# Adding gathered rows four gathers later, with seven row buffers, in the last stage of a transformer block

## The chip, the cores and the metric

One core of a Trainium2 chip runs the whole program. The metric is the device time of one execution in microseconds (us), the median of several runs. The core has five engines with a queue of instructions each: TensorE (PE, with PEld for its weight loads), VectorE (DVE), ScalarE (ACT), GpSimd (POOL) and SyncE (SP, which only issues DMAs here). Each engine takes its instructions in their order, and waits at one whose inputs or buffers are not ready.

## The reference

The program is one layer of a streaming encoder over 256 tokens of width 2048: two mixers, an output projection, and then a layer of very many small experts (PEER), and a final normalisation. The last stage computes the output half of the experts:

```
eidx, gate = top 16 of 128 x 128 experts, for each of 8 heads     # 128 experts for each token
a  = einsum('td,thkd->thk', x, emb_u[eidx])
w  = gelu(a) * gate
y  = einsum('thk,thkd->td', w, emb_v[eidx])                       # the last stage
x  = x + ga2 * y
out = rmsnorm(x, norm_f_g)
```

`emb_v` has 16384 rows of 2048 float32 numbers, 134 MB.

## The kernel before, in words

Tokens lie on partitions in two groups of 128 (`tt` is 0 or 1). The stages up to the experts' weights are not touched by the change. What is left is y, and the columns of y are computed in two ways side by side.

Columns 576 to 2047 (`GV` = 1472 of them) are a dense product. An earlier step scattered the weights w into a table `W` (the same memory as `A`), 128 blocks of 128 experts by 256 tokens, zero where a token did not choose an expert. For each of the 128 blocks (`NK`) `v_load` brings 128 rows of the table `v_cols` by an SP DMA into a buffer `vb` (three of them, 736 KB each) and splits them into a high and a low part: ACT casts `vb` to `vh` (L1079), DVE subtracts to get `vl` (L1081). The weights of the block are split the same way (`wh` L1075, `wl` L1077). `vh` and `vl` have two buffers each. The PE then does 18 matmuls a block, in three runs of six, `wh` x `vh`, `wl` x `vh` and `wh` x `vl` (`product`, L1131): they add into six banks `yp` over all 128 blocks. A `vb` buffer is free for the next load once its `vl` is written.

Columns 0 to 575 (`GW` = 576) are gathered: for each of the 256 pairs of a token group and one of its 128 chosen experts, an indirect DMA issued from POOL (`gather`, L755) fetches a row for each of the 128 tokens into a buffer `gat`, and DVE multiplies it with the weight and adds it to `yg` (L1064, L1062 for the first of a group). In `weigh`, before, both are one step: the gather is recorded and then its addition. There are five `gat` buffers, and a new gather waits for the addition that read its buffer.

The main loop runs over blocks i. It records the load and split of block i + 1, then the products of block i, then two gathers with their additions (256 gathers over 124 blocks are 2.06 a block). Each gather is held back until the last product of block i (`after=mm`). The order in which each engine meets the work is set by the program's scheduler, which keeps the dependencies and otherwise goes by a priority that follows the recorded order.

At the end (`residual` and `finish`) DVE multiplies `yg` and `yp` with `ga2`, adds x, and after a normalisation SP stores the result.

Of the kernel before, what the change touches and what calls it, by code (L numbers as in the profile page):

```python
# [10 lines left out]
F32 = mybir.dt.float32  # L11
F32R = mybir.dt.float32r
# [3 lines left out]
AF = mybir.ActivationFunctionType  # L16
ALU = mybir.AluOpType
PACE = mybir.DependencyInfo(mybir.DependencyClass.Sync, mybir.DependencyReason.DATA)
AX = mybir.AxisListType
PSUM = bass.MemoryType.PSUM  # L20

P = 128
T = 256
# [37 lines left out]
GW = 576  # L61
ON_POOL = ((0, 3), (1, 3))
BACK, ENDS = NK - 5, 4
COLS = 2 * NK - 50
GV = D - GW

# [48 lines left out]
def block_kernel(ctx, tc, a, out):  # L115
    nc = tc.nc
    def pool(name, side, bufs=1, space=None):
        stack = ExitStack()
        kw = {} if space == bass.MemoryType.DRAM else {"reuse_waits": "tile"}
        if space is not None:  # L120
            kw["space"] = space
        return stack.enter_context(tc.tile_pool(name=name, bufs=bufs, side=side, **kw)), stack

    keep, keep_s = pool("keep", "left")
# [3 lines left out]
    late = {}  # L128
# [26 lines left out]
    first = sb.tile([P, 4 * D], F32, tag="oT", name="first")  # L155
# [11 lines left out]
    def rsqrt(dst, src, scale):  # L167
        nc.vector.tensor_scalar(dst, src, scale, EPS, op0=ALU.mult, op1=ALU.add)
        nc.vector.reciprocal(dst, dst)
        nc.scalar.activation(dst, dst, AF.Sqrt)  # L170
# [121 lines left out]
    def first_products(j, w, parts, last=False, after=None):  # L292
        for part in parts:
            for c in range(3):
                for tt in range(TT):
                    acc, ww, cs = (qacc[c * TT + tt], w[0], c * WIDE) if c < 2 else (kacc[tt], w[1], 0)
                    for k in range(2):
# [3 lines left out]
                        if after is not None:  # L301
                            tc.add_manual_dep(mm.ins, after.ins.name, PACE, reason="the modulation first")

# [392 lines left out]
    u_rows, u_cols, v_rows, v_cols = a["peer_u_rows"], a["peer_u_cols"], a["peer_v_rows"], a["peer_v_cols"]  # L696
# [16 lines left out]
    def norm2():  # L713
        drain()
        nc.sync.dma_start(ga2d, adaR[96:97])
        ssum = late["ssum"] = keep.tile([P, TT], F32, name="ssum")
        nc.vector.tensor_reduce(ssum, late["ss"], axis=AX.X, op=ALU.add)
        rsqrt(ssum, ssum, 1.0 / D)
# [29 lines left out]
    def rows_of(name):  # L748
        return pe[name].rearrange("p t h k -> p t (h k)")
# [3 lines left out]
    def gather(pool_, tag, table, width, bufs, tt, n, after=None, room=None):  # L753
        g = pool_.tile([P, room or width], F32, tag=tag, bufs=bufs, name="gat")[:, :width]
        d = nc.gpsimd.indirect_dma_start(out=g, out_offset=None, in_=table,  # L755
                                         in_offset=bass.IndirectOffsetOnAxis(ap=rows_of("idx")[:, tt, n:n + 1], axis=0))
        if after is not None:
            tc.add_manual_dep(d.ins, after.ins.name, PACE, reason="gathers spread over the products")
        return g
# [12 lines left out]
    todo = [(tt, n) for hs in range(0, HEADS, 2) for tt in range(TT) for n in range(hs * TOPK, (hs + 2) * TOPK)]  # L772
# [8 lines left out]
    def route_post(h):  # L781
        def post(ps):
# [61 lines left out]
            nc.gpsimd.tensor_tensor(oh, oh, idf.rearrange("p t q k -> p (t q) k")[:, :, None, :].to_broadcast(every), op=ALU.mult)  # L844
            nc.vector.tensor_reduce(got, oh.rearrange("p (t q) k a -> p t q k a", q=2), axis=AX.X, op=ALU.add)
            nc.vector.scalar_tensor_tensor(pe["idx"][:, :, h], got[:, :, 0], float(NK), got[:, :, 1], op0=ALU.mult, op1=ALU.add)
# [11 lines left out]
    drain()  # L858
    i12 = pe["i12"].rearrange("p t q h k -> p q t (h k)")
    idx, gate = rows_of("idx"), rows_of("gate")  # L860
    colT = keep.tile([P, 4, T], F32, name="colT")
    i1T, i2T, wT, gT = (colT[:, i] for i in range(4))
    wrow = pe["wrow"]
    neg = keep.tile([P, T], F32, name="neg")
    idr = keep.tile([P, P], F32R, name="idr")

    def softmax():
        ex = pe["gate"]
# [3 lines left out]
        nc.scalar.activation(ex, ex, AF.Exp)  # L872
        nc.vector.tensor_reduce(sm, ex, axis=AX.X, op=ALU.add)
        nc.vector.reciprocal(sm, sm)
        nc.vector.tensor_tensor(ex, ex, sm[:, :, :, None].to_broadcast([P, TT, HEADS, TOPK]), op=ALU.mult)

    def columns():
        softmax()
        nc.scalar.copy(idr, ident)
        for dst, src in ((i1T, i12[:, 0]), (i2T, i12[:, 1]), (gT, gate)):  # L880
            pt = bank("pt")
            for tt in range(TT):
                nc.tensor.transpose(pt[:, tt * P:(tt + 1) * P], src[:, tt], ident)
            nc.scalar.copy(dst, pt[:, :T])
            if dst is i2T:
                nc.scalar.mul(neg, pt[:, :T], -1.0)
# [23 lines left out]
    for n in range(DIRECT):  # L910
        mm = u_products(n)
    late["pg_s"].close()
    st_s.close()
    big, big_s = pool("big", "left")
    A = big.tile([P, NK, T], F32, tag="big", name="A")

    rate = (len(todo) - LEFT) / (2 * NK - PRE)
    done = 0
    for n in range(2 * NK):
        if n >= DIRECT:  # L920
            mm = u_products(n)
        if n % 4 == 3:
            nc.scalar.copy(A[:, n // 2 - 1:n // 2 + 1], sums.pop(n // 4))
        if n == COLS:
            columns()
# [49 lines left out]
    def pick(u):  # L975
        for h in range(2):
# [3 lines left out]
            for t in range(4):  # L980
                mm = nc.tensor.matmul(pkv[:, t], oh[:, t], A[:, :, t0 + t], start=True, stop=True)
                tc.declare_no_dep(mm.ins, group="scattered", reason="other tokens' columns")
# [11 lines left out]
    def scatter(u):  # L994
# [3 lines left out]
        for h in range(0, SET, 4):  # L998
            pw, pwv = psum("pw", 3)
            for t in range(4):  # L1000
                nc.tensor.matmul(pwv[:, t], o2[:, h + t].bitcast(F32), o1[:, h + t], start=True, stop=True)  # L1001
            put = nc.scalar.copy(A[:, :, t0 + h:t0 + h + 4].rearrange("p n t -> p t n"), pwv)  # L1002
            tc.add_to_no_dep_group("scattered", put.ins)
# [20 lines left out]
    for u in range(-LEAD, units + LAG):  # L1024
        if 0 <= u < units and u % half == 0:
            tt = u // half
# [18 lines left out]
        if 0 <= u < units and u % half == half - 1:  # L1045
            pt, _ = psum("pk", 3)
            nc.tensor.transpose(pt[:, :P], wT[:, tt * P:(tt + 1) * P], ident)
            nc.vector.tensor_copy(wrow[:, tt], pt[:, :P])
    W = A

    p2_s.close()
    pq_s.close()
    py, py_s = pool("py", "left", bufs=1, space=PSUM)
    psc, psc_s = pool("psc", "left", bufs=2, space=PSUM)
    p3, p3_s = pool("p3", "right")

    yg = p3.tile([P, TT, GW], F32, name="yg")
    def weigh(tt, n, after=None):
        g = gather(p3, "gat", v_rows, GW, 5, tt, n, after)
        w = wrow[:, tt, n:n + 1]  # L1060
        if n == 0:
            nc.vector.tensor_scalar(yg[:, tt], g, w, None, op0=ALU.mult)  # L1062
        else:
            nc.vector.scalar_tensor_tensor(yg[:, tt], g, w, yg[:, tt], op0=ALU.mult, op1=ALU.add)  # L1064

    todo = list(pairs)
    chunks = [(c, min(512, GV - c)) for c in range(0, GV, 512)]
# [2 lines left out]
    def v_load(i):  # L1070
        room, bufs = (p3, 1) if i % 3 == 2 else (pv, 2)
        vb = room.tile([P, GV], F32, tag="vb", bufs=bufs, name="vb")
        nc.sync.dma_start(vb, v_cols[i * P:(i + 1) * P])
        wh = p3.tile([P, T], F32R, tag="wh", bufs=3, name="wh")
        nc.scalar.copy(wh, W[:, i])  # L1075
        wl = p3.tile([P, T], F32R, tag="wl", bufs=3, name="wl")
        nc.vector.tensor_tensor(wl, W[:, i], wh.bitcast(F32), op=ALU.subtract)  # L1077
        vh = p3.tile([P, GV], F32R, tag="vh", bufs=2, name="vh")
        nc.scalar.copy(vh, vb)  # L1079
        vl = p3.tile([P, GV], F32R, tag="vl", bufs=2, name="vl")  # L1080
        late["split"] = nc.vector.tensor_tensor(vl, vb, vh.bitcast(F32), op=ALU.subtract)  # L1081
        return vh, vl, wh, wl

    spent = A.rearrange("p n t -> p (n t)")
    x1 = spent[:, :TT * D].rearrange("p (t d) -> p t d", t=TT)
# [7 lines left out]
    def restore(after):  # L1093
# [6 lines left out]
        for d in loads:  # L1100
            tc.add_manual_dep(d.ins, after.ins.name, PACE, reason="behind the last of the table")

    def residual(tt, m):
        c, w, n = parts[m]
        xs = xo[:, tt, c:c + w]
        mul = nc.vector.tensor_tensor(xs, yg[:, tt] if n is None else yp[tt][n][:, :w], ga2[:, c:c + w], op=ALU.mult)  # L1106
        tc.add_manual_dep(mul.ins, late["split"].ins.name, PACE, reason="the last operands first")
        (nc.gpsimd if (tt, m) in ON_POOL else nc.vector).tensor_tensor(xs, xs, x1[:, tt, c:c + w], op=ALU.add)  # L1108
        nc.scalar.activation(sq[:, :w], xs, AF.Square, accum_out=ss3[:, tt, m:m + 1])
        if n is None:  # L1110
            nc.gpsimd.tensor_tensor(xs, xs, gf[:, c:c + w], op=ALU.mult)

    def finish(tt):
        for m in range(len(chunks)):
            residual(tt, m)
        r = rf[:, tt:tt + 1]
        nc.vector.tensor_reduce(r, ss3[:, tt], axis=AX.X, op=ALU.add)
        rsqrt(r, r, 1.0 / D)
# [18 lines left out]
    for i in range(NK - 2):  # L1137
        ops = nxt
        nxt = v_load(i + 1)
        for j in range(3):  # L1140
            for tt in range(TT):
                for n in range(len(chunks)):
                    mm = product(i, ops, j, tt, n)
        while todo and done < rate * (i + 1):
            weigh(*todo.pop(0), after=mm)
            done += 1
        if i == BACK:
            restore(mm)
    ends = [nxt, v_load(NK - 1)]
    for tt in range(TT):  # L1150
        residual(tt, len(parts) - 1)
    for tt in range(TT):
# [61 lines left out]
```

## Time and profile before

| | us |
|---|---|
| three runs | 2393.7, 2394.3, 2401.22 |
| median | 2394.3 |
| span of the profiled execution | 2393.9 |
| last stage, from the first `vh` cast (1803.31) to the end | 590.6 |

The page gives no other time for the profiled execution than its span. In the page's first part an engine's busy time and its share of the span stand side by side: PE 2208.9 us (92%), DVE 1785.1 us (75%), ACT 1031.0 us (43%), POOL 874.9 us (37%). These are means over stages with different limits. In a row of a group of instructions the numbers after the bar are the time in which at least one of them ran, the mean duration of one in ns, and the idle time of that engine just before them with what ended it. In a timeline a row is a start, a duration, an engine, a line and an operation, and in brackets the time its engine stood idle before it and what ended that.

### The profile page before, as it was taken

To read this page: it belongs to the slowest core of one execution; us is meant where nothing else is said; L and a number is where in the kernel's file an instruction comes from. 1 tells how busy PE (TensorE), PEld (TensorE's weight loads), DVE (VectorE), ACT (ScalarE), POOL (GpSimd) and SP (SyncE) were. 2 spreads that over 40 slices of the span, in tenths; PEclk is the share of its full clock that TensorE was granted. 3 is DMA by queue.
4 is the path that set the end of the run, shared out by engine and by line. 5 is a ranking of instruction groups with operands and counts; after the bars stand their busy time and mean duration, and the time that the engine had idled before them with its cause. 6 is when DMAs were issued, how large, how long until landed. Compare 5 with 4: busy or idle time off the path is not lost. (4 is left out here: it accounts for less than half of the span.)

```text
span 2393.9 us, 37307 instructions
## 1 busy us (share of the span) xinstructions
PE 2208.9 (92%) x13988; PEld 1949.2 (81%) x13988; DVE 1785.1 (75%) x3416; ACT 1031.0 (43%) x1440; POOL 874.9 (37%) x750
## 2 busy tenths in 40 slices
PE   6999999999999998893999999989998998998996
PEld 3577779999999888783889999989997777777775
DVE  3478878888788755787767777777766877877777
ACT  3245556643344444101444444457774333333333
POOL 0000000000000002766444444467775665666664
PEclk9999999999999999996999999999999999999998
DMA  9977778777777765767999999971107888888987
GB/s 353 380 296 265 273 267 297 276 286 283 285 295 282 264 213 180 257 224 221 302 302 313 318 316 313 305 248 54 33 1 253 310 301 297 304 306 299 313 310 269
DMA packets 144312, 638.26 MB, mean 267 GB/s; under 512 B 20721, under 2 KB 26625, under 8 KB 112001
## 3 DMA queue, kind: packets, MB, share of 16 engines
q1 hardware_dynamic: 102146, 459.65, 53.7%
q0 software_dynamic: 41984, 176.23, 21.8%
q8 instruction: 109, 1.79, 0.3%
q14 instruction: 73, 0.60, 0.1%
HBM read 631.59 MB, written 4.20 MB: 266 GB/s over the span
## 5 line engine op out<-in xcount | busy, mean ns | idle before, releaser
L755 POOL DMA_INDIRECT gat<-in_peer_v_rows,eidx x256 | 351.4, 1373 | 211.3 <-PE yp L1131 138.7
L755 POOL DMA_INDIRECT gat<-in_peer_u_rows,eidx x256 | 315.0, 1230 | 301.8 <-DVE ulo L710 146.2
L211 ACT CAST whi<-wt 128x2048 fp32r<-128x2048 f32 x130 | 248.0, 1908 | 292.4 <-PE mm L412 224.4
L906 PE MATMUL mmu<-h2T,uhi 128*128 128x256 f32 x2360 | 323.9, 284 | 33.6 <-ACT uhi L709 33.6
L762 DVE SCALAR_TENSOR_TENSOR gat<-gat,h2b 128x768 f32<-128x768 f32 x256 | 245.1, 959 | 142.9 <-DMA gat<-in_peer_u_rows,eidx 141.6
L213 DVE TENSOR_TENSOR wlo<-wt,whi 128x2048 fp32r<-128x2048 f32 (+1 forms) x130 | 292.3, 2249 | 55.5 <-ACT whi L211 51.6
L906 PEld LDWEIGHTS mmu<-h2T,uhi 128*128 128x128 f32 x2360 | 301.8, 193 | 34.4 <-ACT uhi L709 34.4
L1079 ACT CAST vh<-vb 128x1472 fp32r<-128x1472 f32 x128 | 182.9, 1429 | 340.6 <-DMA vb<-in_peer_v_cols 289.4
L356 POOL DMA_DIRECT2D br<-in_b_ada x32 | 15.8, 493 | 773.2 <-DVE ada_acc L357 726.8
L1064 DVE SCALAR_TENSOR_TENSOR yg<-gat,wrow,yg 128x576 f32<-128x576 f32 x254 | 207.5, 817 | 113.0 <-DMA gat<-in_peer_v_rows,eidx 110.8
L709 ACT CAST uhi<-ub 128x640 fp32r<-128x640 f32 x236 | 171.5, 728 | 268.3 <-DMA ub<-in_peer_u_cols 220.8
L1131 PE MATMUL yp<-vl,wh 128*128 128x512 f32 (+1 forms) x768 | 201.3, 396 | 45.9 <-DVE vl L1081 45.0
L353 DVE SCALAR_TENSOR_TENSOR ada_acc<-wa,sc_col,ada_acc 128x256 f32<-128x256 f32 x480 | 231.7, 483 | 11.4
L1081 DVE TENSOR_TENSOR vl<-vb,vh 128x1472 fp32r<-128x1472 f32 x128 | 215.6, 1684 | 6.6 <-ACT vh L1079 6.6
L906 PE MATMUL mmu<-h2T,ulo 128*128 128x256 f32 x1180 | 188.1, 290 | 32.1 <-DVE ulo L710 30.7
L1131 PEld LDWEIGHTS yp<-vl,wh 128*128 128x128 f32 x768 | 139.1, 189 | 96.0 <-DVE vl L1081 72.8
L906 PEld LDWEIGHTS mmu<-h2T,ulo 128*128 128x128 f32 x1180 | 158.2, 192 | 45.8 <-DVE ulo L710 44.7
L1131 PE MATMUL yp<-vh,wh 128*128 128x512 f32 (+1 forms) x768 | 192.2, 384 | 2.6 <-ACT wh L1075 2.6
L710 DVE TENSOR_TENSOR ulo<-ub,uhi 128x640 fp32r<-128x640 f32 x236 | 188.8, 820 | 6.2 <-ACT uhi L709 5.8
L1131 PE MATMUL yp<-vh,wl 128*128 128x512 f32 (+1 forms) x768 | 191.4, 383 | 0.1
L412 PE MATMUL mm<-whi,hT 128*128 128x512 f32 (+1 forms) x832 | 181.7, 362 | 0.0
L1131 PEld LDWEIGHTS yp<-vh,wh 128*128 128x128 f32 x768 | 145.0, 189 | 28.4 <-ACT wh L1075 2.8
(275 smaller groups left out, 3696.2 us busy)
## 6 DMA issues: line engine op xcount, KB each, us to landing
wa<-in_w_ada SPq DMA_DIRECT2D x96, 1024.0 KB
vb<-in_peer_v_cols SPq DMA_DIRECT2D x128, 736.0 KB
ub<-in_peer_u_cols SPq DMA_DIRECT2D x256, 320.0 KB
wt<-in_w_vg SPq DMA_DIRECT2D x32, 1024.0 KB
wt<-in_w_branch_gate SPq DMA_DIRECT2D x32, 1024.0 KB
wt<-in_w_u SPq DMA_DIRECT2D x16, 1024.0 KB
wt<-in_w_b_out SPq DMA_DIRECT2D x16, 1024.0 KB
wt<-in_w_o SPq DMA_DIRECT2D x16, 1024.0 KB
```

The costliest lines, as they stand in the source:

```text
L211: nc.scalar.copy(hi, wt)
L213: nc.vector.tensor_tensor(lo[:, :cut], wt[:, :cut], hi[:, :cut].bitcast(F32), op=ALU.subtract)
L353: nc.vector.scalar_tensor_tensor(acc, wt[:, k], s, acc, op0=ALU.mult, op1=ALU.add)
L412: nc.tensor.matmul(job.ps[b], l, r, start=(first and k == 0 and i == 0 and not lo_part), stop=(last and k == job.rows - 1 and lo_part == 1))
L710: (nc.gpsimd if n < POOL else nc.vector).tensor_tensor(lo[:, :w], ub[:, :w], hi[:, :w].bitcast(F32), op=ALU.subtract)
L755: d = nc.gpsimd.indirect_dma_start(out=g, out_offset=None, in_=table, in_offset=bass.IndirectOffsetOnAxis(ap=rows_of("idx")[:, tt, n:n + 1 ...
L762: nc.vector.scalar_tensor_tensor(g, g, 1.0, h2b[:, tt, :UG], op0=ALU.mult, op1=ALU.mult, accum_out=pe["wrow"][:, tt, n:n + 1])
L906: mm = nc.tensor.matmul(acc, w[:, k - k0], x, start=(first and k == 0 and i == 0), stop=(last and k == FK - 1 and i == len(steps) - 1))
L1064: nc.vector.scalar_tensor_tensor(yg[:, tt], g, w, yg[:, tt], op0=ALU.mult, op1=ALU.add)
L1079: nc.scalar.copy(vh, vb)
L1081: late["split"] = nc.vector.tensor_tensor(vl, vb, vh.bitcast(F32), op=ALU.subtract)
L1131: return nc.tensor.matmul(yp[tt][n][:, :w], l[:, tt * P:(tt + 1) * P], r[:, c:c + w], start=(i == 0 and j == 0), stop=(i == NK - 1 and j = ...
```

## The change

A gather and its addition are parted. `fly` issues the gather and puts it on a list; `weigh` takes the oldest of the list and adds it, and is called while more than `BEHIND` = 4 gathers are on the list. So in block i the additions are those of the gathers that were issued two blocks before. An ordering edge without a semaphore (`QUEUED`) puts each addition behind `late["split"]`, the `vl` of block i + 1. The buffers `gat` are seven in place of five (2304 bytes a partition each). Their room comes from three tables of the stage before (`colT`, `neg`, `idr`, 4096 + 1024 + 512 bytes a partition), which now lie in a pool of their own that is closed before the last stage. What is still on the list after the loop is added behind the load of the last block.

```diff
+VG, BEHIND = 7, 4
...
-    colT = keep.tile([P, 4, T], F32, name="colT")
-    i1T, i2T, wT, gT = (colT[:, i] for i in range(4))
-    neg = keep.tile([P, T], F32, name="neg")
-    idr = keep.tile([P, P], F32R, name="idr")
...
+    pick_room, pick_room_s = pool("pickroom", "left")
+    colT = pick_room.tile([P, 4, T], F32, name="colT")
+    i1T, i2T, wT, gT = (colT[:, i] for i in range(4))
+    neg = pick_room.tile([P, T], F32, name="neg")
+    idr = pick_room.tile([P, P], F32R, name="idr")
...
+    pick_room_s.close()
...
-    def weigh(tt, n, after=None):
-        g = gather(p3, "gat", v_rows, GW, 5, tt, n, after)
+    flying = []
+
+    def fly(tt, n, after):
+        flying.append((gather(p3, "gat", v_rows, GW, VG, tt, n, after), tt, n))
+
+    def weigh():
+        g, tt, n = flying.pop(0)
         w = wrow[:, tt, n:n + 1]
         if n == 0:
-            nc.vector.tensor_scalar(yg[:, tt], g, w, None, op0=ALU.mult)
+            d = nc.vector.tensor_scalar(yg[:, tt], g, w, None, op0=ALU.mult)
         else:
-            nc.vector.scalar_tensor_tensor(yg[:, tt], g, w, yg[:, tt], op0=ALU.mult, op1=ALU.add)
+            d = nc.vector.scalar_tensor_tensor(yg[:, tt], g, w, yg[:, tt], op0=ALU.mult, op1=ALU.add)
+        tc.add_manual_dep(d.ins, late["split"].ins.name, QUEUED, reason="the split of the next block first")
...
         while todo and done < rate * (i + 1):
-            weigh(*todo.pop(0), after=mm)
+            fly(*todo.pop(0), after=mm)
             done += 1
+        while len(flying) > BEHIND:
+            weigh()
         if i == BACK:
             restore(mm)
     ends = [nxt, v_load(NK - 1)]
+    while flying:
+        weigh()
```

DVE's queue before, in the middle of the stage. `vl_19133` and `vl_19167` belong to blocks 40 and 41; `gat_19085` and `gat_19088` are the two gathers held back until the last product of block 37, `gat_19119` and `gat_19122` those of block 38, `gat_19153` the first of block 39.

```order
L1064 SCALAR_TENSOR_TENSOR yg_17770<-gat_19085,wrow_8619,yg_17770 128x576
L1064 SCALAR_TENSOR_TENSOR yg_17770<-gat_19088,wrow_8619,yg_17770 128x576
L1081 TENSOR_TENSOR vl_19133<-vb_19125,vh_19131 128x1472
L1077 TENSOR_TENSOR wl_19163<-A_9902,wh_19161 128x256
L1064 SCALAR_TENSOR_TENSOR yg_17770<-gat_19119,wrow_8619,yg_17770 128x576
L1064 SCALAR_TENSOR_TENSOR yg_17770<-gat_19122,wrow_8619,yg_17770 128x576
L1081 TENSOR_TENSOR vl_19167<-vb_19159,vh_19165 128x1472
L1077 TENSOR_TENSOR wl_19197<-A_9902,wh_19195 128x256
L1064 SCALAR_TENSOR_TENSOR yg_17770<-gat_19153,wrow_8619,yg_17770 128x576
```

The same place of DVE's queue now. The `vl` of a block has the same number; the gathers of block 37 are `gat_19085` and `gat_19087`, those of block 38 `gat_19119` and `gat_19121`, and `vl_19201` belongs to block 42.

```order
L1091 TENSOR_TENSOR vl_19133<-vb_19125,vh_19131 128x1472
L1073 SCALAR_TENSOR_TENSOR yg_17774<-gat_19085,wrow_8619,yg_17774 128x576
L1087 TENSOR_TENSOR wl_19163<-A_9899,wh_19161 128x256
L1073 SCALAR_TENSOR_TENSOR yg_17774<-gat_19087,wrow_8619,yg_17774 128x576
L1091 TENSOR_TENSOR vl_19167<-vb_19159,vh_19165 128x1472
L1073 SCALAR_TENSOR_TENSOR yg_17774<-gat_19119,wrow_8619,yg_17774 128x576
L1087 TENSOR_TENSOR wl_19197<-A_9899,wh_19195 128x256
L1073 SCALAR_TENSOR_TENSOR yg_17774<-gat_19121,wrow_8619,yg_17774 128x576
L1091 TENSOR_TENSOR vl_19201<-vb_19193,vh_19199 128x1472
```

The gathers of block 37 stood ahead of the `vl` of block 40 and now stand behind it; those of block 38 stood ahead of the `vl` of block 41 and now stand ahead of that of block 42. Each `vl` waits for gathers that were issued one block earlier than before, and an addition now stands on each side of the `wl`.

The end of DVE's queue before: the last two additions and the last two `vl`, then the first step of the residual.

```order
L1064 SCALAR_TENSOR_TENSOR yg_17770<-gat_22024,wrow_8619,yg_17770 128x576
L1064 SCALAR_TENSOR_TENSOR yg_17770<-gat_22027,wrow_8619,yg_17770 128x576
L1081 TENSOR_TENSOR vl_22070<-vb_22062,vh_22068 128x1472
L1077 TENSOR_TENSOR wl_22094<-A_9902,wh_22092 128x256
L1081 TENSOR_TENSOR vl_22098<-vb_22090,vh_22096 128x1472
L1106 TENSOR_TENSOR A_9902<-yg_17770,A_9902 128x576 x2
```

And now (`vl_22098` is the `vl` of the last block, `gat_21990` and `gat_21992` the first two of the last four gathers):

```order
L1091 TENSOR_TENSOR vl_22070<-vb_22062,vh_22068 128x1472
L1087 TENSOR_TENSOR wl_22094<-A_9899,wh_22092 128x256
L1091 TENSOR_TENSOR vl_22098<-vb_22090,vh_22096 128x1472
L1073 SCALAR_TENSOR_TENSOR yg_17774<-gat_21990,wrow_8619,yg_17774 128x576
L1116 TENSOR_TENSOR A_9899<-yg_17774,A_9899 128x576
L1073 SCALAR_TENSOR_TENSOR yg_17774<-gat_21992,wrow_8619,yg_17774 128x576
```

The last four additions moved behind the last `vl`, in among the steps of the residual. On POOL, SP and PE the order in the stage is as it was (the stores of the result come in another order). On ACT the cast that fills `idr` moved from the start of the program, with a table load of its own, to the stage that needs it.

## Rows read from the trace of the kernel before

**Rows 1.** Page: the chain that ended last, by line, shares of the span.

```profile
DMA gat<-in_peer_v_rows,eidx 12%; POOL gat L755 3%; DVE yg L1064 2%; DVE vl L1081 1%; PE yp L1131 1%; DMA vb<-in_peer_v_cols 1%; DVE wl L1077 0%; DVE A L1108 0%; ACT vh L1079 0%; DVE A L1106 0%; DVE A L1124 0%; POOLq L755 0%; PE pw L1001 0%; ACT A L1002 0%; DVEq L1064 0%
```

**Rows 2.** Windows: busy time of each engine from 1850 to 2250 us.

```profile
core 0: us, PE busy (x) PEld busy (x) DVE busy (x) ACT busy (x) POOL busy (x), PEclk, DMA share, GB/s
1850.00:2250.00 400.00, 367.48 (x1605) 297.66 (x1604) 316.27 (x363) 153.15 (x177) 253.86 (x186) 1.00 0.88 304
```

**Rows 3.** Groups by line, 1850 to 2340 us: busy, mean ns, idle before.

```profile
L755 POOL DMA_INDIRECT gat<-in_peer_v_rows,eidx x226 | 312.9, 1384 | 180.4 <-PE yp L1131 124.8 <-issue 25.0 <-DVE yg L1064 20.8
L1081 DVE TENSOR_TENSOR vl<-vb,vh 128x1472 fp32r<-128x1472 f32 x110 | 185.2, 1684 | 0.0
L1064 DVE SCALAR_TENSOR_TENSOR yg<-gat,wrow,yg 128x576 f32<-128x576 f32 x224 | 183.0, 817 | 101.2 <-DMA gat<-in_peer_v_rows,eidx 99.3
L1131 PE MATMUL yp<-vl,wh 128*128 128x512 f32 (+1 forms) x654 | 170.6, 396 | 39.6 <-DVE vl L1081 38.8 <-issue 0.2
...
L1079 ACT CAST vh<-vb 128x1472 fp32r<-128x1472 f32 x109 | 155.7, 1429 | 298.2 <-DMA vb<-in_peer_v_cols 258.9 <-PE yp L1131 23.4 <-DVE yg L1064 6.9
```

**Rows 4.** Timeline: the `vl` of block 5 and that of block 125.

```profile
1827.47 1.74 DVE L1081 TENSOR_TENSOR vl<-vb,vh 128x1472 fp32r<-128x1472 f32 x1
...
2364.03 1.69 DVE L1081 TENSOR_TENSOR vl<-vb,vh 128x1472 fp32r<-128x1472 f32 x1
```

**Rows 5.** Timeline, 1977 to 1997 us: a gather that keeps PE waiting.

```profile
1978.48 1.48 PE L1131 MATMUL yp<-vh,wh 128*128 128x512 f32 x6
1978.84 1.68 DVE L1081 TENSOR_TENSOR vl<-vb,vh 128x1472 fp32r<-128x1472 f32 x1
...
1978.92 2.43 POOL L755 DMA_INDIRECT gat<-in_peer_v_rows,eidx  x1 [2.70 <-PE yp L1131]
...
1981.65 0.95 POOL L755 DMA_INDIRECT gat<-in_peer_v_rows,eidx  x1 [0.30 <-DVE yg L1064]
...
1982.44 1.48 PE L1131 MATMUL yp<-vh,wh 128*128 128x512 f32 x6
...
1987.48 0.82 DVE L1064 SCALAR_TENSOR_TENSOR yg<-gat,wrow,yg 128x576 f32<-128x576 f32 x1 [3.10 <-DMA gat<-in_peer_v_rows,eidx]
...
1989.55 0.82 DVE L1064 SCALAR_TENSOR_TENSOR yg<-gat,wrow,yg 128x576 f32<-128x576 f32 x1 [1.25 <-DMA gat<-in_peer_v_rows,eidx]
1990.29 1.69 DVE L1081 TENSOR_TENSOR vl<-vb,vh 128x1472 fp32r<-128x1472 f32 x1
...
1992.03 2.82 PE L1131 MATMUL yp<-vl,wh 128*128 128x512 f32 x6 [2.82 <-DVE vl L1081]
```

**Rows 6.** The matmuls of L1131, 1850 to 2340 us: idle time before them.

```profile
  DVE vl L1081: 38.8, 45
```

**Rows 7.** Chain in order of time: longest `vb` load, longest gather (start, us).

```profile
2026.21 7.19 DMA vb<-in_peer_v_cols
...
2155.04 8.73 DMA gat<-in_peer_v_rows,eidx
```

**Rows 8.** DMA, GB/s in 40 slices of 1850 to 2340 us.

```profile
GB/s 298 315 309 321 317 282 325 281 319 303 290 261 320 285 338 307 311 285 304 301 311 295 310 305 313 293 303 283 326 285 320 328 300 303 308 308 326 300 292 317
```

**Rows 9.** Page: GB/s in 40 slices of the whole span.

```profile
GB/s 353 380 296 265 273 267 297 276 286 283 285 295 282 264 213 180 257 224 221 302 302 313 318 316 313 305 248 54 33 1 253 310 301 297 304 306 299 313 310 269
```

**Rows 10.** Tile gat, 1850 to 2340 us: POOL's durations, ns min/median/max.

```profile
L755 POOL DMA_INDIRECT gat<-in_peer_v_rows,eidx x226: 940/1268/2476, 1848.5 to 2338.2; - x113
```

**Rows 11.** Timeline of the start and the end of the program.

```profile
15.22 1.94 PE L268 MATMUL acc<-wa,sc_rep 128*32 128x256 f32 x16 [15.22 <-DMA wa<-in_w_ada]
...
2369.16 0.82 DVE L1064 SCALAR_TENSOR_TENSOR yg<-gat,wrow,yg 128x576 f32<-128x576 f32 x1 [2.38 <-DMA gat<-in_peer_v_rows,eidx]
2369.90 1.68 DVE L1081 TENSOR_TENSOR vl<-vb,vh 128x1472 fp32r<-128x1472 f32 x1
...
2371.84 1.68 DVE L1081 TENSOR_TENSOR vl<-vb,vh 128x1472 fp32r<-128x1472 f32 x1
...
2373.55 1.43 DVE L1106 TENSOR_TENSOR A<-yg,A 128x576 f32<-128x576 f32 x2
```

More of the change, by code (lines that the diff above doesn't have):

```diff
@@ L18 @@
 PACE = mybir.DependencyInfo(mybir.DependencyClass.Sync, mybir.DependencyReason.DATA)
+QUEUED = mybir.DependencyInfo(mybir.DependencyClass.NoSync, mybir.DependencyReason.DATA)
 AX = mybir.AxisListType
```

## The prediction

> **What bounds the kernel now.** I read the chain of waits first. Of its lines that belong to the last stage the gather `gat` is by far the longest, with 12% of the whole span; the DVE and PE lines beside it have 1 to 3% [rows 1]. So the stage is set by something that hangs on the gathers' landing, while the page's first part has PE at 92% and would point elsewhere.
>
> The window of 400 us in the middle of the stage comes next [rows 2]: PE busy 92%, DVE 79%, POOL 63%, ACT 38%, the DMA engines 88%, the granted clock 1.00. No engine is full, so waits decide. How long a block takes: from the `vl` of block 5 to that of block 125 are 120 blocks in 2364.03 - 1827.47 = 536.56 us, 4.471 us each [rows 4]. How long it would take if PE never waited: in the timeline a run of six matmuls starts at 1978.48 and the run three runs later at 1982.44, so a block's 18 take 3.96 us, 1.32 a run [rows 5]. PE loses 0.511 us a block, 61.3 us over the 120.
>
> Where it loses them: the groups of the stage show PE idle before one run only, that of `wh` x `vl`, for 38.8 us [rows 3], in 45 waits [rows 6]; the six matmuls after such a wait are also longer (2.82 us in rows 5, where others take 1.48), and there I put the rest. DVE, which writes `vl`, stood idle 99.3 us for gathers and not at all before `vl` itself [rows 3]. The timeline shows how one becomes the other [rows 5]. The last product of block 38 is issued just before 1978.48; POOL issues its two gathers from 1978.92 and 1981.65; they are added at 1987.48 and 1989.55, after DVE waited 3.10 and 1.25 us; only then comes the `vl` of block 41, 1990.29 to 1991.97, and PE, which waits for it, goes on at 1992.03. Without a wait PE would have been there two blocks and two runs after 1978.48, at 1978.48 + 7.92 + 2.64 = 1989.04.
>
> **The change part by part.** *The order on DVE.* The gathers of block 38 now stand ahead of the `vl` of block 42, no longer of block 41. In the same case the second addition starts at 1989.55 and takes 0.82, and the `vl` behind it ends at 1989.55 + 0.82 + 1.68 = 1992.05. PE wants it three blocks and two runs after 1978.48: 1978.48 + 11.88 + 2.64 = 1993.00. It is in time by 0.95 us where it was late by 2.99. This is one of the late gathers (its first wait of 3.10 is three times the mean, 99.3 us over some hundred waits), so I take the wait of PE for `vl` as gone in nearly every block. The `wl` that now stands behind the first addition is needed only one run into block 42, at 1978.48 + 11.88 + 1.32 = 1991.68; it could run from 1988.30, so this costs nothing.
>
> What is late next. DVE's own work: 79% of 4.471 is 3.53 us a block [rows 2], below 3.96. POOL: 2.06 gathers at 1.384 and 0.30 between them [rows 3, 5] are 3.47 us, below 3.96. The `vb` buffers: from a `vl` that frees one, the longest load in the chain takes 7.19 us [rows 7], the cast 1.43 and the next `vl` 1.68 [rows 3], 10.30 in all, and three buffers allow 3 x 3.96 = 11.88. That ACT idles 258.9 us for `vb` [rows 3] is therefore no wait of PE. What stands closest is the DMA rate: 304 GB/s x 4.471 us = 1359 KB a block [rows 2]. At 3.96 us this asks for 343 GB/s. The best slice of 12 us of this stage has 338 [rows 8], which would give 1359 / 338 = 4.02 us; the best slice of the kernel has 380 [rows 9], which would give 3.58 and leave PE the bound. These are the two ends, 4.02 and PE's 3.96; I take 4.02, since the row of 338 has this stage's mix of transfers. The gain is (4.471 - 4.02) x 120 = 54.1 us.
>
> The Trainium skill (DMA: Bandwidth & Descriptors, Specifications) gives a core about 358 GB/s from the HBM. The slice of 380 goes beyond that, and the trace decides; with 358 a block's loads would take an estimated 3.80 us, PE would bound at 3.96, and the gain would be 61.3 us.
>
> *The end.* The last four additions come after the last `vl`, 4 x 0.817 = 3.3 us [rows 3], among the residual's steps, where DVE has no gap from 2369.90 on [rows 11]. Against it stands DVE's wait of 2.38 us for the last gather ahead of `vl` of block 126 [rows 11], which goes. The net is between -2.4 (if the additions fit into DVE's waits for PE's last products) and +3.3 us; I take +3.3, as DVE's row there is full.
>
> *The seven buffers.* Gathers waited 20.8 us for an addition to free a buffer [rows 3]; with seven this should not grow although additions come two gathers later. Worth nothing by itself, as the same row shows POOL idle 124.8 us for PE's pacing. If the cover fails, a gather starts later by up to the 20.8 us over 110 blocks, 0.19 us each, below the 0.95 us to spare.
>
> *The moved tables.* The cast of `idr` and its table load leave the start of ACT, but PE's first product waits there for the DMA of `wa` until 15.22 [rows 11], so nothing comes of it; a cast more in the later stage is a fraction of a us. Bounds 2 us either way, taken as 0.
>
> **The sum.** 2393.9 (span; 0.4 below the median) - 54.1 + 3.3 = 2343.1, say 2343. With 3.96 us a block and the end at -2.4 it is 2330. What this leaves out is the first blocks, whose first `vl` still stands behind a gather, and which the 120 blocks don't hold.
>
> **The rivals.**
> *Fuller DMA queues make gathers later.* With the DMA engines at 88% and rising, landing times grow. The longest gather in the chain takes 8.73 us from POOL [rows 7]; the case above took 1987.48 - 1981.35 = 6.1 for its first. If the typical late one comes 2 us later, `vl` is ready 1992.05 + 2 - 1978.48 = 15.57 after the issue, which has to fit into three blocks and 2.64 us: 4.31 us a block, a gain of 19.3, 2378. For it: the rate has to go up by an eighth. Against it: 0.95 us are to spare even in a late case, and the `vb` loads become evenly spaced.
>
> *The DMA rate is full already.* If 304 GB/s is what this mix gives, blocks stay at 4.471, DVE waits less and ACT more, and with the end 2393.9 + 3.3 = 2397: no change. Against it: the slices range from 261 to 338 [rows 8], so the rate follows demand.
>
> *POOL becomes the bound: slower.* Issuing a gather takes POOL 940 ns at least and 2476 at most [rows 10]. The one of 2.43 us in the timeline lay under a `vl` from 1978.84 to 1980.52 [rows 5]. With DVE's work denser, and an addition and the `vl` taking turns, more issues can fall under a `vl`. POOL takes over from PE's pace when 2.06 x (mean + 0.30) passes 3.96, at a mean of 1.62, and the kernel gets slower than before from 2.06 x (mean + 0.30) = 4.471, a mean of 1.87. If half the issues took 2.43 and half today's 1.384, 1.91, a block would be 4.55 us: +9.5 and the end's 3.3, 2407. If all took 2.476, 5.72 us, 2547. Against it: the mean is 1.384 today with `vl` on for 38% of the time, and that share would only rise to 42%.
>
> The Trainium skill (SBUF — State Buffer, Who interferes with whom) states that a DVE instruction with two SBUF inputs contends with a GpSimd instruction that reads SBUF, and that the loser waits for the other's end. `vl` and the additions are of that kind. The trace agrees for `vl` by the row of 2.43 us. By this rule the additions should hold an issue as well, for at most their 0.82 us, and the rival's 2407 could be reached.
>
> **How the numbers follow.** Chances: the forecast (2330 to 2362) 0.62; later gathers (2362 to 2387) 0.21; rate already full (2387 to 2401) 0.07; POOL as the bound, or another way to be slower, 0.10. I count 0.3% (7 us) as what a measurement of this kernel can tell from no change. Nearly all of the first two cases is faster: 0.83; same 0.08; slower 0.09. The range that leaves out 2 in 10 goes from 2330 to 2385; the forecast's own is 2330 to 2362.
>
> **What would show it.** Right: the `vl` of a block every 4.0 to 4.05 us; no idle time of PE before `wh` x `vl` beyond a few us; the DMA at 335 GB/s or more in the same stretch; DVE still waiting for gathers, but in the place of idle time and without PE behind it; the line `gat` in the chain given way to PE's `yp` or the `vb` load. Wrong: 45 or so waits of PE as before, or PE waiting for `vh` in their place (then `vb` loads bound), or POOL's mean issue beyond 1.6 us. A time above 2387 would mean that DMA or POOL hold the stage.

## The result, and the profile after

The changed kernel takes 2358.9 us in the median (2354.8 to 2363.9, four runs) against 2395.7 of the kernel before on the same chip: a ratio of 0.985, 95% interval [0.983, 0.987]. Faster, as forecast, inside the range of 2330 to 2385, but by 36.8 us where the forecast had 51. Each kernel of the experiments was measured beside the kernel before on its own chip, where that one's median was 2390.6 to 2396.4 us; so medians of different chips compare to some 6 us.

The profiled executions differ by 2393.9 - 2362.1 = 31.8 us, and the `vl` of block 5, the `vl` of block 125 and the end of the span divide them into three parts (timeline rows of the changed kernel; those of before are in [rows 4]):

```profile
1828.16 1.68 DVE L1091 TENSOR_TENSOR vl<-vb,vh 128x1472 fp32r<-128x1472 f32 x1
...
2327.75 1.68 DVE L1091 TENSOR_TENSOR vl<-vb,vh 128x1472 fp32r<-128x1472 f32 x1
```

The 120 blocks take 499.6 us in place of 536.6, 4.163 us each in place of 4.471: 37.0 us gained. Up to block 5 it is 0.7 us later. From block 125 to the end it takes 34.4 us in place of 29.9: 4.5 us lost.

The window from 1850 to 2250 us, after, answers to [rows 2]:

```profile
core 0: us, PE busy (x) PEld busy (x) DVE busy (x) ACT busy (x) POOL busy (x), PEclk, DMA share, GB/s
1850.00:2250.00 400.00, 389.14 (x1731) 323.48 (x1731) 335.92 (x390) 167.39 (x194) 322.16 (x201) 1.00 0.93 328
```

PE, DVE and the DMA rate rose with the pace, by some 6 to 8%. POOL rose by 27%, from 253.9 to 322.2 us. The groups of that window show the reason. They answer to [rows 3], which cover 90 us more; PE's row of before in the same 400 us stands ahead of them:

```profile
L1131 PE MATMUL yp<-vl,wh 128*128 128x512 f32 x534 | 139.3, 396 | 32.5 <-DVE vl L1081 32.2
```
```profile
L757 POOL DMA_INDIRECT gat<-in_peer_v_rows,eidx x201 | 326.1, 1622 | 78.1 <-issue 32.0 <-PE yp L1141 22.4 <-DVE wl L1087 18.6
...
L1073 DVE SCALAR_TENSOR_TENSOR yg<-gat,wrow,yg 128x576 f32<-128x576 f32 x197 | 160.4, 814 | 63.1 <-DMA gat<-in_peer_v_rows,eidx 57.4 <-issue 4.4 <-DVE vl L1091 0.4
L1141 PE MATMUL yp<-vl,wh 128*128 128x512 f32 (+1 forms) x576 | 145.5, 388 | 10.8 <-DVE vl L1091 9.0 <-issue 1.6
```

PE's idle time before `wh` x `vl` fell from 32.5 to 10.8 us, but an issue of a gather takes 1622 ns in place of 1384, and POOL hardly waits for PE any more (22.4 us, where it was 124.8 in the 490 us of [rows 3]). Most of its idle time of 78.1 us is the 0.30 us between one issue and the next: 201 x (1.622 + 0.30) = 386 us of 400. POOL is nearly full.

The tile's durations, min/median/max, answer to [rows 10]:

```profile
L757 POOL DMA_INDIRECT gat<-in_peer_v_rows,eidx x239: 940/1297/3097, 1847.2 to 2326.6; - x120
```

The longest issue was 2476 ns and is 3097 now. Of the 256 issues of the stage 39 are longer than 2.6 us; before there was none. They are the whole rise: the mean of the others is 1.369 us, and that of all was 1.373 before. The timeline shows two of them:

```profile
2312.93 0.81 DVE L1073 SCALAR_TENSOR_TENSOR yg<-gat,wrow,yg 128x576 f32<-128x576 f32 x1
2313.66 0.42 DVE L1087 TENSOR_TENSOR wl<-A,wh 128x256 fp32r<-128x256 f32 x1
2313.99 0.81 DVE L1073 SCALAR_TENSOR_TENSOR yg<-gat,wrow,yg 128x576 f32<-128x576 f32 x1
2314.14 3.09 POOL L757 DMA_INDIRECT gat<-in_peer_v_rows,eidx  x1 [0.31 <-DVE wl L1087]
2314.72 1.68 DVE L1091 TENSOR_TENSOR vl<-vb,vh 128x1472 fp32r<-128x1472 f32 x1
2316.32 0.81 DVE L1073 SCALAR_TENSOR_TENSOR yg<-gat,wrow,yg 128x576 f32<-128x576 f32 x1
2317.05 0.42 DVE L1087 TENSOR_TENSOR wl<-A,wh 128x256 fp32r<-128x256 f32 x1
2317.39 0.81 DVE L1073 SCALAR_TENSOR_TENSOR yg<-gat,wrow,yg 128x576 f32<-128x576 f32 x1
2317.53 3.10 POOL L757 DMA_INDIRECT gat<-in_peer_v_rows,eidx  x1 [0.30 <-DVE wl L1087]
2318.12 1.68 DVE L1091 TENSOR_TENSOR vl<-vb,vh 128x1472 fp32r<-128x1472 f32 x1
...
2320.93 0.95 POOL L757 DMA_INDIRECT gat<-in_peer_v_rows,eidx  x1 [0.30 <-DVE wl L1087]
...
2323.11 0.82 DVE L1073 SCALAR_TENSOR_TENSOR yg<-gat,wrow,yg 128x576 f32<-128x576 f32 x1 [2.23 <-DMA gat<-in_peer_v_rows,eidx]
```

An issue begins some 0.14 us after the start of the addition that stands in front of `vl`, and ends 0.82 us after the end of that `vl` (2314.72 + 1.68 + 0.82 = 2317.22). The next issue begins 0.30 us later, at 2317.53, which is again 0.14 us into the addition in front of the next `vl`. An issue of 3.09 us and its 0.30 make 3.39 us, the time in which DVE goes once through `vl`, addition, `wl`, addition. So the two keep step: one issue for each turn of DVE, where 2.06 a block are needed. The step doesn't last. DVE uses two gathers a turn and soon has to wait for one, 2.23 us here; the 39 long issues are 16 pairs and 7 single ones, never three on end.

How narrow the case is, the starts of all issues within that addition show. Of 40 that began 0.13 to 0.15 us into it 39 were long. None of the 26 that began 0.16 to 0.76 us into it was: 24 of them ended 0.82 us after the addition. The 4 that began within its first 0.1 us took 0.95 us, as an issue does that nothing holds. Why an issue at 0.14 us is held through the `vl` too, no run shows.

The end, in the chain of waits: SP issues the load of the final gain row behind block 123, and the chain goes through it.

```profile
2327.36 17.24 DMA A<-in_norm_f_g
2344.60 0.02 issue
2344.64 0.08 issue
2344.74 1.40 POOL A L1121
2346.13 1.74 POOL A L1118
```

The residual's operands are 4 MB, asked for at once right behind the last `vb` load. The part on the change says that POOL's order in the stage is as it was; at its end it is not. POOL's queue now holds the product with the gain of one token group (L1121) ahead of the other group's addition (L1118). Before, both additions (L1108) stood ahead of both products (L1111), and POOL waited 0.59 us for the gain row where it now waits 3.97:

```profile
2374.45 3.64 POOL L1108 TENSOR_TENSOR A<-A 128x576 f32<-128x576 f32 x2 [11.44 <-DVE A L1106]
2378.68 3.19 POOL L1111 TENSOR_TENSOR A<-A 128x576 f32<-128x576 f32 x2 [0.59 <-DMA A<-in_norm_f_g]
```

### The profile page after: what moved, and what is told of

It is laid out like the page before. It is cut to its first block, busy times and chain, and to the rows that moved or that the text cites. A ratio compares the mean times of both kernels' runs of the same rounds, so it can differ in the third digit from the quotient of the medians.

```text
span 2362.1 us, 37306 instructions
## 1 busy us (share of the span) xinstructions
PE 2199.1 (93%) x13988; PEld 1953.3 (83%) x13988; DVE 1779.2 (75%) x3416; ACT 1028.9 (44%) x1439; POOL 938.0 (40%) x750
## 5 line engine op out<-in xcount | busy, mean ns | idle before, releaser
L757 POOL DMA_INDIRECT gat<-in_peer_v_rows,eidx x256 | 417.3, 1630 | 106.6 <-issue 40.2
L355 DVE SCALAR_TENSOR_TENSOR ada_acc<-wa,sc_col,ada_acc 128x256 f32<-128x256 f32 x480 | 231.7, 483 | 11.4
L1091 DVE TENSOR_TENSOR vl<-vb,vh 128x1472 fp32r<-128x1472 f32 x128 | 215.7, 1685 | 11.4 <-ACT vh L1089 11.3
L904 PE MATMUL mmu<-h2T,ulo 128*128 128x256 f32 x1180 | 189.4, 291 | 34.4 <-DVE ulo L712 33.5
L1141 PE MATMUL yp<-vl,wh 128*128 128x512 f32 (+1 forms) x768 | 195.4, 388 | 14.1 <-DVE vl L1091 12.2
```

What stands on the lines that cost most here:

```text
L355: nc.vector.scalar_tensor_tensor(acc, wt[:, k], s, acc, op0=ALU.mult, op1=ALU.add)
L904: mm = nc.tensor.matmul(acc, w[:, k - k0], x, start=(first and k == 0 and i == 0), stop=(last and k == FK - 1 and i == len(steps) - 1))
L1141: return nc.tensor.matmul(yp[tt][n][:, :w], l[:, tt * P:(tt + 1) * P], r[:, c:c + w], start=(i == 0 and j == 0), stop=(i == NK - 1 and j = ...
```

## The experiments

My first theory after the result: POOL's issue bounds the changed kernel, lengthened by DVE's work beside it. The rival: the DMA rate, as the prediction had it, at 328 GB/s in place of 338.

**The buffers alone.** The kernel before, seven buffers for five (the three tables are moved as in the change; that part is left out here):

```diff
-        g = gather(p3, "gat", v_rows, GW, 5, tt, n, after)
+        g = gather(p3, "gat", v_rows, GW, 7, tt, n, after)
```

> The kernel before with seven row buffers in place of five and the three tables moved, nothing else: each gather is still added ahead of the next block's split. If the order on VectorE is what counts, this is as before: 2395 us within 7, a block every 4.47 us, and some 45 waits of TensorE for vl in the middle of the stage. If the buffers are what brings the gain (the gathers waited 20.8 us for a free one), it comes near the changed kernel's 2359.

Measured: 2392.8 us, ratio 0.999 [0.996, 1.001]; a block takes 4.452 us, and PE still waits for `vl`, 30.3 us in the window where it was 32.5:

```profile
L1133 PE MATMUL yp<-vl,wh 128*128 128x512 f32 x538 | 139.3, 394 | 30.3 <-DVE vl L1083 29.7
```

The buffers alone bring nothing that could be measured.

**More DMA in the changed kernel.**

```diff
         nc.sync.dma_start(vb, v_cols[i * P:(i + 1) * P])
+        if 10 <= i < BACK - 3:
+            nc.sync.dma_start(W[:, i - 10], v_cols[i * P:(i + 1) * P, :T])
```

> The changed kernel with one more DMA of 128 KB in each of 110 blocks (rows of the table, into a part of W that is used up; nothing reads it), 1487 KB a block in place of 1359. If GpSimd's issue of the gathers bounds (in the changed kernel's trace it is busy or in the 0.30 us between two issues for 96% of the stage, its mean issue 1630 ns against 1384 before), the DMA engines can take it: the best slice of the changed kernel's stage shows 367 GB/s, 1487/367 = 4.05 us a block, so the time rises by less than 15 us over 2359. If the DMA rate of 328 GB/s is full, a block takes 1487/328 = 4.53 us and the time is 2359 + 0.37 x 110 = 2400.

Measured: 2369.5 us, ratio to before 0.987 [0.982, 0.992], which overlaps with the changed kernel's. The medians differ by 10.6 us; in the profiled executions 5.2 of 11.2 us lie ahead of block 5, where nothing was changed. A block takes 4.220 us. In the same window:

```profile
1850.00:2250.00 400.00, 384.42 (x1702) 319.80 (x1701) 329.92 (x383) 163.23 (x189) 317.80 (x194) 0.99 0.98 353
```

353 GB/s: the 328 were not the DMA engines' limit. With 9% more bytes a block took 1.4% longer.

**Both additions behind `wl`.** The order wl, addition, addition, vl, with the lag of four kept:

```diff
-        nc.vector.tensor_tensor(wl, W[:, i], wh.bitcast(F32), op=ALU.subtract)
+        d = nc.vector.tensor_tensor(wl, W[:, i], wh.bitcast(F32), op=ALU.subtract)
+        if late.get("split") is not None:
+            tc.add_manual_dep(d.ins, late["split"].ins.name, QUEUED, reason="behind the last on this engine")
+        while i < NK - 1 and len(flying) > BEHIND:
+            d = weigh(d)
...
         late["split"] = nc.vector.tensor_tensor(vl, vb, vh.bitcast(F32), op=ALU.subtract)
+        tc.add_manual_dep(late["split"].ins, d.ins.name, QUEUED, reason="behind the last on this engine")
...
```

(`weigh` puts its addition behind `d` and returns it; its call in the main loop is gone.)

> The changed kernel with another order on VectorE, the lag of four gathers kept: a block's two additions stand side by side behind the wl, as in the kernel before (wl, addition, addition, vl), in place of one on each side of the wl. If the issues of 3.1 us on GpSimd come from its start falling in step with the addition in front of vl, they go, the mean issue returns to about 1.4 us, GpSimd no longer bounds, and a block takes 3.96 to 4.05 us: 2337 to 2347. If the DMA rate bounds at 4.16 us, it stays at 2359 within 7. If GpSimd is held by VectorE's density in any order, the mean issue stays at 1.6 and so does the time.

Measured: 2341.0 us, ratio to the kernel before 0.977 [0.973, 0.982], 18 us below the changed kernel. A block takes 3.969 us, which is PE's own 3.96. Window and groups:

```profile
1850.00:2250.00 400.00, 399.30 (x1813) 339.72 (x1812) 356.29 (x410) 173.87 (x202) 262.69 (x208) 1.00 0.96 343
```
```profile
L757 POOL DMA_INDIRECT gat<-in_peer_v_rows,eidx x208 | 262.7, 1263 | 138.3 <-PE yp L1147 96.7 <-issue 22.1 <-DVE yg L1073 19.5
...
L1147 PE MATMUL yp<-vl,wh 128*128 128x512 f32 (+1 forms) x601 | 149.0, 383 | 0.2 <-issue 0.2
```

PE is busy 399.3 of 400 us. POOL moves more gathers in 18% less time, waits for PE again (96.7 us), and the mean issue is 1263 ns; one of 256 is longer than 2.6 us. DVE's work is the same, and denser: 356 us. So it is not how much DVE works beside an issue that lengthens it, but in which order. The timeline shows where the order acts:

```profile
1912.26 1.69 DVE L1096 TENSOR_TENSOR vl<-vb,vh 128x1472 fp32r<-128x1472 f32 x1
1912.62 2.15 POOL L757 DMA_INDIRECT gat<-in_peer_v_rows,eidx  x1 [0.30 <-issue]
...
1913.86 0.42 DVE L1088 TENSOR_TENSOR wl<-A,wh 128x256 fp32r<-128x256 f32 x1
...
1914.20 1.67 DVE L1073 SCALAR_TENSOR_TENSOR yg<-gat,wrow,yg 128x576 f32<-128x576 f32 x2
1915.07 0.94 POOL L757 DMA_INDIRECT gat<-in_peer_v_rows,eidx  x1 [0.30 <-DVE yg L1073]
1915.78 1.69 DVE L1096 TENSOR_TENSOR vl<-vb,vh 128x1472 fp32r<-128x1472 f32 x1
```

An issue held by a `vl` ends 0.82 us after it here too (1914.77), and the next begins 0.30 us later. But a turn of DVE takes 3.52 us in place of 3.39, so the addition in front of the next `vl` starts later, at 1915.05, and the issue comes 0.02 us into it in place of 0.14. Of the 45 issues that follow a held one into that addition here, 44 came within its first 0.05 us and took 0.95 us; of the 48 in the changed kernel 39 were long. So what the order moves is a phase of about 0.1 us. No run moves that phase and nothing else.

**Fewer issues on POOL.** Every eighth gather as a plain load on SP:

```diff
+        if n % 8 == 7:
+            g = p3.tile([P, GW], F32, tag="gat", bufs=VG, name="gat")
+            nc.sync.dma_start(g, v_rows[n * P:(n + 1) * P])
+        else:
+            g = gather(p3, "gat", v_rows, GW, VG, tt, n, after)
```

> The changed kernel with every eighth gather replaced by a plain load of as many bytes on SyncE's queue (fixed rows, so the choice of these rows is left out): the same bytes, the same additions in the same order, 12.5% fewer issues on GpSimd. If GpSimd's issue bounds, a block needs 1.81 x 1.93 = 3.49 us of it, and the next bound shows: 3.96 to 4.05 us a block, 2337 to 2347. If the DMA rate bounds, 2359 within 7.

Measured: 2351.2 us, ratio to before 0.982 [0.978, 0.986], 4.100 us a block. In the right direction, but 7.8 us where the theory of a full engine gave 12 to 22, and the interval overlaps with the changed kernel's.

```profile
L757 POOL DMA_INDIRECT gat<-in_peer_v_rows,eidx x176 | 305.0, 1733 | 96.6 <-PE yp L1146 43.1 <-issue 20.2 <-DVE wl L1092 19.2
```

With fewer issues their mean rose to 1733 ns: 47 of 224 are longer than 2.6 us, where it was 39 of 256, again at most two on end. POOL is no longer full, 305 + 176 x 0.30 = 358 us of 400, and yet PE waits 8.6 us for `vl` and a block takes 4.100 us. So a full POOL is not all of it. A long issue also makes its own gather and the ones behind it late: in the changed kernel's trace 35 of 59 late additions (waits over 0.3 us), with 47.7 of their 68.0 us, have a long issue as their own or among the two before it, which holds for a third of all gathers, and each of PE's 19 waits for `vl` stands behind an addition that waited. So it is likely, though no run shows it by itself, that this lateness is why the order gained more than the count.

**Five buffers in the changed kernel.**

```diff
-VG, BEHIND = 7, 4
+VG, BEHIND = 5, 4
```

> The changed kernel, its order and its lag of four, with five row buffers in place of seven. A gather then waits for the addition of the gather five before it, and that one is added four gathers after its own issue. If the buffers are needed for the lag, POOL idles for additions (DVE yg as the releaser) and the time goes up from 2359 towards 2395 (each wait starts a gather later, by about a us). If the lag alone brings the gain, 2359 within 7.

Measured: 2370.5 us, ratio to before 0.990 [0.987, 0.993], 4.245 us a block, 11.5 above the changed kernel, between the two cases that were expected. The lag without the two buffers keeps two thirds of the gain; POOL idles 19.9 us for additions in the window, where it was 4.6 with seven. 49 issues are long here and 39 were there, so the buffers may not be all of the difference.

**Additions with one input less.** The changed kernel's order; the sum over the experts is left out:

```diff
-            d = nc.vector.scalar_tensor_tensor(yg[:, tt], g, w, yg[:, tt], op0=ALU.mult, op1=ALU.add)
+            d = nc.vector.tensor_scalar(yg[:, tt], g, w, None, op0=ALU.mult)
```

> The changed kernel, its order kept, with every addition but the first replaced by a product alone (yg = row x weight: the sum over the experts is left out), so that it has one input in SBUF beside the weights and is shorter. If an addition with two inputs in SBUF holds POOL's issue, and so makes the issues of 3.1 us together with the vl behind it, these go and no issue is longer than about 2.5 us; POOL's mean falls to 1.4 and the time to 2337 to 2350. If any work of VectorE there holds it, issues of about 2.8 us stay.

Measured: 2341.1 us, 3.986 us a block. The tile's durations:

```profile
L757 POOL DMA_INDIRECT gat<-in_peer_v_rows,eidx x234: 945/1050/2827, 1848.5 to 2298.1; - x117
L1073 DVE TENSOR_SCALAR yg<-gat,wrow x233: 503/519/762, 1849.6 to 2299.4; 128x576 f32<-128x576 f32 x117
```

The issues of 3.09 us are gone, the mean is 1350 ns in the window and the gain is that of the other order. Both signs of the expectation came in part: two of 256 issues are longer than 2.6 us, at most 2.83. The second input is not what decides. Of 30 issues that began 0.12 to 0.36 us into one of these products, with its one input beside the weights, 29 ended 0.81 to 0.89 us after it, as behind an addition. What differs is the length, 519 ns for 814: 24 of the issues behind a held one now miss the short product, begin as the `vl` does and take some 2.49 us, held by the `vl` alone. So the phase changed here too.

**The end: loads earlier, additions back, loads spread.** Four kernels on top of the one with the other order. First the restore loads 19 blocks earlier:

```diff
-BACK, ENDS = NK - 5, 4
+BACK, ENDS = NK - 24, 4
```

> The kernel of e4 (both additions side by side behind wl) with the loads of the residual's operands 19 blocks earlier (BACK = NK - 24 in place of NK - 5). In the changed kernel's trace POOL waits 11.7 us for x1 and 4.0 us for the row of the final gain, and the chain ends on that load. If the end is held by these loads, the stretch from the vl of block 125 to the end falls from 34.4 us to 30 or less, and the time from 2341 to 2336. If it is held by VectorE with its four late additions, it stays at 34.

Measured: 2351.5 us, 10.5 above. The end fell from 34.4 to 30.4 us, about as expected, but the time rose, since in the middle of the stage PE stood still (timeline):

```profile
2244.55 1.60 PE L1147 MATMUL yp<-vl,wh 128*128 128x512 f32 x6
2257.51 2.82 PE L1147 MATMUL yp<-vh,wh 128*128 128x512 f32 x6 [11.36 <-ACT vh L1094]
```

4 MB, four loads issued one behind the other, stand ahead of the next `vb` load on SP's queue. PE waits 11.4 us at once here, and the 120 blocks take 491.4 us in place of 476.3, more than the 4.0 us that the end gained. I had not thought of this queue when I wrote what to expect.

Then also the last four additions ahead of the `vl` of blocks 126 and 127:

```diff
-        while i < NK - 1 and len(flying) > BEHIND:
+        while len(flying) > min(BEHIND, 2 * (NK - 1 - i)):
```

> The kernel of e6 with the last four additions ahead of the vl of blocks 126 and 127, as in the kernel before. If the four additions behind the last vl cost what was put on them, 3.3 us, this is 3 us below e6, or more, as POOL then also has the order of before at the end; if their gathers land late there, PE waits for the last vl and it is no better than e6.

Measured: 2349.3 us; the end takes 28.4 us, 2.0 less than without it, where 3 or more were expected. The medians differ by 2.2, less than the two intervals tell apart.

The next kernel has the same edit of that line, and leaves the loads behind block 123 (`BACK = NK - 5`).

> The kernel of e4 with the last four additions ahead of the vl of blocks 126 and 127, the loads of the residual's operands left where they were (behind block 123). In e9 the end, from the vl of block 125 on, was 28.4 us against 34.4 in e4, but the loads moved forward in one piece cost 11 us of TensorE's time. If the four additions and POOL's order at the end make the longer end, it falls to 30 and the time is 4 us below e4's 2341. If the loads make it, the end stays at 33 to 34.

Measured: 2335.5 us, ratio to before 0.976 [0.973, 0.979], which overlaps with the 0.977 of the run without this edit; end 30.7 us, 3.7 less than with the additions behind the last `vl`. POOL again has both additions ahead of both products. So, with the loads where they were, the four additions and POOL's order make 3.7 of the 4.5 us by which the end had grown. The two effects don't add: with the loads early the same edit gave 2.0, and the loads alone had given 4.0.

The last one adds to it that the 4 MB come in pieces of 256 KB, one behind every sixth block from block 24 on (`restore` issues the next piece; that part is left out here):

```diff
-        if i == BACK:
+        if again and i >= 24 and i % 6 == 0:
             restore(mm)
```

> The kernel of e11 with the residual's operands loaded in 16 pieces of 256 KB, one behind every sixth block from block 24 on, in place of 4 MB at once. The DMA rate a block needs goes from 343 to 354 GB/s; e3 ran at 353. If there is room, blocks stay at 3.97 us, the end falls to 28.5 and the time to about 2335. If the DMA engines are full at that rate, blocks go to 4.05 us and the gain at the end is lost: 2341 to 2344.

Measured: 2331.1 us, ratio to before 0.975 [0.972, 0.978], end 28.9 us, 3.964 us a block:

```profile
1850.00:2250.00 400.00, 399.25 (x1812) 339.51 (x1811) 356.11 (x408) 173.63 (x201) 260.49 (x208) 1.00 0.97 353
```

353 GB/s with PE busy 399 of 400 us. This is the fastest kernel found: 28 us below the changed one by the medians, and some 23 by the ratios (0.975 and 0.985), as the kernel before was 5 us faster on this chip. Its interval overlaps that of the run without spread loads.

## Why the prediction was right, and where its sizes were off

The time lies even in the forecast's narrower range, 2330 to 2362, but that is in part luck: the range stood on the DMA rate or PE as the next bound, and what held the blocks back was POOL, the rival that had a chance of 0.10 and was priced at 2407. Of the signs that the prediction named, PE's waits fell and DVE still waits for gathers. But a block took 4.163 us, not 4.0 to 4.05, the DMA ran at 328 GB/s, not 335, `gat` is still the longest line of the chain (8% of the span, `yp` 4%), and a sign of being wrong came: a mean issue of POOL beyond 1.6 us.

*The order on DVE* held. Each `vl` waits for gathers one block older, and PE's idle time before `wh` x `vl` fell from 32.5 us in the window to 10.8. With the lag but without POOL's trouble (the run with both additions behind `wl`) it fell to 0.2, and the block to 3.969 us: of the 61.3 us of gain that were read from PE's own pace the 120 blocks of that run give 60.2.

*The DMA rate as the next bound* was the step that failed. The prediction took the best slice of the stage, 338 GB/s, for a limit, and 4.02 us a block. The rate was not a limit: 343, 344 and 353 GB/s were reached with PE full. The Trainium skill (DMA: Bandwidth & Descriptors, Specifications) has about 358 GB/s for a core. By it PE would have been the bound, as it was once the order was changed. Over the 400 us no run went above it, though slices of 10 us did, up to 402 GB/s in the last run.

*POOL: 3.47 us a block, below 3.96* was the term that was mis-sized, and it decided. It was worked out with the mean issue of before, 1.384 us. The issue took 1.622 in its place, and 2.06 x (1.622 + 0.30) = 3.96 us, no longer below PE's pace. With POOL occupied 386 of 400 us that is 4.10 a block, where 4.163 was measured. The rival named the mechanism and the point (POOL takes over from a mean of 1.62), but I priced it only for the case in which the kernel gets slower, and argued it away by the share of time with a `vl` on. That share went from 38% to 40% and explains nothing: the lengthening came from the phase. In the order before, when an issue ended 0.82 us behind a `vl` and the next followed it into the addition in front of the next `vl`, that one began within the addition's first 0.05 us and took 0.95 in 9 of 11 cases; now it begins 0.14 us into it and is held through the `vl` in 39 of 48.

The Trainium skill (SBUF — State Buffer, Who interferes with whom) says that a DVE instruction with two SBUF inputs contends with a GpSimd instruction that reads SBUF, and calls the ports that they share an exclusive lock. The traces agree in kind: issues end a fixed 0.82 us after a `vl` or an addition, and none of the 57 that began within the first 0.1 us of the addition in front of `vl` (4 in the changed kernel, 53 with both additions behind `wl`) was held by it. They go further in one point: an issue that began 0.13 to 0.15 us into the addition did not, but for one of 40, get its turn between it and the `vl` right behind, and took up to 3.10 us in place of at most 2.48.

*The end*: +3.3 forecast, +4.5 measured. Putting the additions back took 3.7 of it, so the size was near. But that edit also gives POOL its old order back, and POOL's new order waits 3.97 us for the gain row, which the prediction took as unchanged. How the 3.7 divides between DVE's additions and POOL's wait no run shows.

*The seven buffers* were taken as worth nothing by themselves, and are (ratio 0.999). Under the lag the kernel with five is 11.5 us slower; the prediction's words that the wait should not grow held with seven and not with five.

*The start and the moved tables*: 0 forecast, 0.7 us in the spans, which is within the spread of the runs.

*Later gathers by fuller queues*, the rival with 0.21, is not what happened. Where an addition waited for its gather, it began on average 5.7 us behind the end of that gather's issue before, and 5.6 us in the changed kernel. At 343 GB/s it was 6.4, so landings do get later, but by less than the rival's 2 us, and the additions wait less there (43.7 us of DVE in the window) than at 328 (63.1).

## What to carry to other kernels

When an in-order engine waits for a load ahead of work that another engine needs, move the consumer of the load behind that work: it was worth 37 us here, and more buffers without it nothing. Before trusting the next bound, ask of every engine whose work is lengthened by its neighbours (GpSimd beside VectorE) what the new order does to the phase between them, not only to the sum of busy times; where two orders are free, try both. Loads that have time should be spread in pieces: the same 4 MB cost PE a wait of 11.4 us in one piece on the queue of the streamed operand, and in sixteen pieces PE idled 0.8 us over the 120 blocks.

## What I had not expected of the hardware

An indirect DMA's issue on GpSimd and VectorE's turn fell into step: an issue of 3.09 us, 0.30 us, and the next at the same point of VectorE's turn of 3.39 us, for two turns and never for three. It hung on about 0.1 us: an issue that began 0.13 to 0.15 us into the addition in front of `vl` took 2.8 to 3.1 us in 39 of 40 cases, one that began earlier in it 0.95 us, and one that began later in it at most 2.5. The order in which VectorE holds the same four instructions moved the mean issue from 1622 to 1263 ns and the kernel by 18 us.
